# Rests of split weights: an adding transfer issued by GpSimd onto a negative written by ScalarE, in place of subtractions on VectorE and GpSimd

## The chip, the cores and the metric

One core of one Trainium2 chip runs the whole program once per launch. The metric is the device time of that launch in microseconds (us); lower is better.

## The reference

Two blocks on a sequence of 1024 rows of width 1024 (batch 1, depth 1), all in float32. The first normalises x, projects it by one wide matrix, runs two gated linear attentions (chunked) and a cross attention over 256 memory rows, gates the result and projects it back. The second is a convolution block with a gated pointwise product, a depthwise convolution of width 31, a LayerNorm and a second pointwise product, and then a hidden layer. Cut to the products by weights:

```python
proj = rms_norm(x, norm_w) @ w_in                       # 1024 x 6160
mkv = rms_norm(mem, mem_norm_w) @ w_mem_kv              # 1024 x 1024
x = rms_norm(x + (mixed * silu(gate)) @ w_out, final)   # 2048 x 1024
u = hl @ w_pw1 + b_pw1                                  # 1024 x 2048
a, g = split(u); u = dwconv(a * sigmoid(g), w_dw) + b_dw
xl = xl + g1 * (silu(layer_norm(u)) @ w_pw2 + b_pw2)    # 1024 x 1024
xl = xl + g2 * (square(relu(h2 @ w1)) @ w2)             # 1024 x 4096 x 1024
out = rms_norm(xl, final_g)
```

## The kernel before, in words

**Split products.** Each float32 operand of a weight product is split into a high part (the value cast to the type float32r) and a rest (the value less its high part), and the product is three matmuls in float32r: high by high, high by rest, rest by high (`mm3`). Activations are split where they are made. Weights are split after they have been loaded.

**Weight tasks.** All weight products except those of the hidden layer are cut into 92 tasks, `Task`. A task has one weight tile of 128 x 2048 float32 (1 MB; 2176 columns in the two tasks with the low-rank gate). The kinds are `in` (input projection), `out`, `kv` (memory), `pw1` and `pw2`. Each task's generator yields after a quarter of its matmuls (about 24 of 256 columns or 12 of 512), a `kv` task after each of its two halves. The loop at the end of `block_kernel` takes task after task from `W.next()`; after each yield it calls `W.tick` and then `service`.

**Class `Weights`.** Three rings of two buffers each hold the loaded tile (`wst`), its high part (`whi`) and its rest (`wlo`). While a task runs, the tile of the next one is split and the one after it is loaded by SyncE. `plan` writes the split as a list of six entries, `todo`. For each half of the tile (1024 columns), `hi(j)` casts the half to `whi` on ScalarE, and two entries `lo` subtract a quarter each (512 columns) into `wlo`. The helper `rest` picks VectorE or GpSimd for each subtraction by a cost model. The very first tile takes another way (`eager`). `tick(done)` issues entries until their share of the list reaches `done`; `next` flushes what is left. So where an entry stands in the order of its engine is set by the number that the loop hands to `tick`: 1.3 times the share of the task that has been issued (2.0 times in the tasks of `pw2` of the second half).

**Order of the other work.** All other work (scores, recurrences, norms, modulation, the convolution) waits in lanes of steps. `service` issues a step when the model's times for its inputs are due and when the model has VectorE and ScalarE no more than 2.0 and 3.5 us ahead of TensorE (`room`, `LIMITS`). The model (`Model.note`) books each instruction under the name of the issuing engine object; only what SyncE issues is booked as a transfer. Each engine then runs its own list in order.

**Hidden layer.** `hidden_layer` comes last and has its own split (`Operands`). It isn't touched.

Every engine operation passes through one helper, so the profile gives line 217 for all; groups are told apart by tiles. In the profile `ps_d` is the PSUM bank ring of the weight products, `hTh`/`hTl`, `mTh`/`mTl` and `acth`/`actl` are high part and rest of activations, `at` a score tile, `macc` an accumulator of the modulation, `osb` an output of the recurrence, `rs`/`rsb` row statistics, and `orc` a reciprocal.

Of the kernel before, what the change touches and what calls it, by code (L numbers as in the profile page):

```python
# [10 lines left out]
F32 = mybir.dt.float32  # L11
# [4 lines left out]
ALU = mybir.AluOpType  # L16
# [207 lines left out]
class Weights:  # L224
# [26 lines left out]
    def plan(self, fast=False):  # L251
        if not self.staged:
            return
        task, st, n = self.staged.pop(0)
        q = n // 4
        box = {}

        def first():
            box["hi"] = self.pool.tile([P, WB], F32R, tag="whi", name="whi")
            box["lo"] = self.pool.tile([P, WB], F32R, tag="wlo", name="wlo")  # L260
            self.ready.append((task.key, box["hi"], box["lo"]))

        def sc(j):
            v = st[:, j * 1024:(j + 1) * 1024].rearrange("p (k c) -> p k c", c=512)
            self.V.tensor_tensor(v, v, task.scale().unsqueeze(1).to_broadcast([P, 2, 512]), op=ALU.mult)

        if self.eager:
            def eager(j):
                if j == 0:
                    first()  # L270
                c = slice(q * j, q * (j + 1))
                self.V.tensor_copy(box["hi"][:, c], st[:, c])
                e = self.G if j < 2 else self.V
                e.tensor_tensor(box["lo"][:, c], st[:, c], box["hi"][:, c].bitcast(F32), op=ALU.subtract)
            self.todo, self.n_todo, self.eager = [lambda j=j: eager(j) for j in range(4)], 4, False
            return

        def hi(j):
            self.A.copy(box["hi"][:, 2 * q * j:2 * q * (j + 1)], st[:, 2 * q * j:2 * q * (j + 1)])

        def lo(j):
            c = slice(q * j, q * (j + 1))
            self.rest(box["lo"][:, c], st[:, c], box["hi"][:, c].bitcast(F32), fast)

        td = []
        for j in range(2):
            if task.scale is not None:
                td.append(lambda j=j: sc(j))
            td.append(lambda j=j: (first() if j == 0 else None, hi(j)))
            td.append(lambda j=j: lo(2 * j))  # L290
            td.append(lambda j=j: lo(2 * j + 1))
        self.todo, self.n_todo = td, len(td)

    def start(self):
# [65 lines left out]
def block_kernel(ctx, tc, x, mem, w_in, w_up, w_kv, w_out, w_mod, w_pw1, w_pw2, w_dw, w_1, w_2,  # L360
# [837 lines left out]
    def less(out, a, b, eng=None):  # L1198
        n = a.free_size()
        v, g = M.free.get("DVE", 0.0) + n / 800.0, M.free.get("POOL", 0.0) + n / 400.0  # L1200
        (eng or (V if v + GAIN < g else G)).tensor_tensor(out, a, b, op=ALU.subtract)

    class Operands:
# [18 lines left out]
        def lo(self, n, eng=None):  # L1222
            t = self.t[n]
            less(t[:, 1, :], self.val(n), t[:, 0, :].bitcast(F32), eng)
            if self.after:
                self.after(n, t)
# [417 lines left out]
    def hidden_layer():  # L1644
# [26 lines left out]
        for c in range(CHUNKS):  # L1671
            for t in range(NT):
                nxt = (c, t + 1) if t < NT - 1 else (c + 1, 0)
                if nxt[0] < CHUNKS:
                    load_s(*nxt)
                out_group(c, t, B0 + 28 * c + 7 * t)
        assert not plan, sorted(plan)


# [156 lines left out]
    W = Weights((V, A, G, DMA, rest), pw, pick)  # L1836
    done = {}

    def mark(ev, *tiles):
        done[ev] = M.time(*tiles) if tiles else M.last  # L1840
# [48 lines left out]
    def due(n):  # L1889

        if not lanes[n]:
            return None
        st = lanes[n][0]
        if any(r not in done for r in st.req):
            return None
        return max([done[r] for r in st.req] + [M.time(*st.need()) if st.need else 0.0] + banks(st.psum))
# [31 lines left out]
    def service(force=False, kind=None):  # L1928

        any_, more = False, True  # L1930
        while more:
            more = False
            for k, e in enumerate(fifo):
                if later_due(e) <= M.now + SLACK:
                    emit_fifo(k)
                    more = True
                    break
            for n in order():
                d = due(n)
                if d is not None and d <= M.now + SLACK and (force or lanes[n][0].rank in URGENT or room(kind)):  # L1940
                    emit(n)
                    more = True
                    break
            any_ = any_ or more
        if force and not any_:
            c = [(due(n), 1, n) for n in lanes if due(n) is not None] + [(later_due(e), 0, k) for k, e in enumerate(fifo)]
            if not c:
                return False
            _, lane_, n = min(c)
            emit(n) if lane_ else emit_fifo(n)  # L1950
        return True

    while True:
        nxt = W.next()
        if nxt is None:
            break
        task, hi, lo = nxt
        if TRACK:
            TRACK["slots"].append((TRACK["pos"][0], round(M.now, 1), task.key))
        while not all(r in done for r in task.req):  # L1960
            if TRACK:
                print("wait", round(M.now, 1), task.key, [r for r in task.req if r not in done],
                      {n: (len(l), l[0].req, due(n)) for n, l in lanes.items() if l}, len(fifo))
            assert service(True), (task.key, [r for r in task.req if r not in done], [(n, l[0].req) for n, l in lanes.items() if l])
        here = 0.0
        for dt in task.go(hi, lo):
            here += dt
            W.tick(min(1.0, (2.0 if task.key[:2] == ("pw2", 1) else 1.3) * here / task.est))
            service(kind=task.key[0])
        if task.ev is not None:  # L1970
            mark(task.ev)
# [62 lines left out]
def build(nc, arrays, dbg=None):  # L2034
    aps = [nc.dram_tensor(f"in_{n}_dram", arrays[n].shape, mybir.dt.from_np(arrays[n].dtype), kind="ExternalInput").ap()
           for n in _ARGS]
    out = nc.dram_tensor("out_0_dram", (S, D), F32, kind="ExternalOutput").ap()
    with tile.TileContext(nc) as tc:
        block_kernel(tc, *aps, out, dbg=dbg)
# [11 lines left out]
```

## Time and profile before

| | |
|---|---|
| time, median of 2 runs | 2038.71 us (2037.25 to 2040.17) |
| the profiled execution | 2043.66 us, of which the span on the core is 2041.6 us |
| busy share of the span | TensorE 96%, VectorE 74%, ScalarE 45%, GpSimd 40% |
| weight tasks | until about 1395 us; the hidden layer follows |
| transfers issued by GpSimd | none |

The span runs from the first to the last instruction of the core. A share of busy time is a mean over stages with different limits. Matmuls overlap in the profile: the end of one is modelled and lies after the start of the next, so a busy TensorE isn't a TensorE at its peak. Idle time is put down to what ended it.

### The profile page before, as it was taken

The page shows a single profiled execution, that of the slowest core. Times are in us where ns is not written, and L with a number is a line of the kernel's source. Part 1 is how long each engine was busy: PE and PEld are TensorE (multiplying, and loading weights), DVE is VectorE, ACT ScalarE, POOL GpSimd, SP SyncE. Part 2 cuts the span into 40 slices and gives each one's busy share as a digit, 9 for nine tenths or more (in the row PEclk, how much of TensorE's full clock was granted, in tenths as well). Part 3 has the DMA queues.
Part 4 walks back from the last instruction along what each step waited for, and adds up shares of the span by engine and source line. Part 5 has one row for each costly group of instructions (what it writes and reads, how often), then busy time and mean ns, then how long its engine had stood idle before and what let it go on. Part 6 is the DMA issues. An engine that isn't in the chain of part 4 may idle for free.

```text
span 2041.6 us, 29949 instructions
## 1 busy us (share of the span) xinstructions
PE 1952.8 (96%) x10892; PEld 1699.0 (83%) x10892; DVE 1504.7 (74%) x2956; ACT 919.5 (45%) x1793; POOL 811.9 (40%) x743
## 2 busy tenths in 40 slices
PE   8999999999999998999899999999999998899998
PEld 6888898789788887878789999997878886688786
DVE  5799777744667877856757676887888778777876
ACT  6433333444623334334424343335777776433343
POOL 3343334344333443343536343650000003877872
PEclk9999999999999999999999999999999999999999
DMA  5242331333123332322433232331699899776765
GB/s 198 68 159 104 114 114 63 144 124 105 45 101 136 123 109 89 133 83 83 141 133 119 71 119 91 117 132 62 179 300 270 245 263 300 264 285 263 268 250 204
DMA packets 177638, 315.05 MB, mean 154 GB/s; under 512 B 9762, under 2 KB 129442, under 8 KB 163794
## 3 DMA queue, kind: packets, MB, share of 16 engines
q1 hardware_dynamic: 175186, 309.33, 44.8%
q10 hardware_dynamic: 2304, 3.80, 0.5%
q8 instruction: 86, 1.41, 0.3%
q14 instruction: 62, 0.51, 0.1%
HBM read 241.78 MB, written 71.31 MB: 153 GB/s over the span
## 4 chain that ended last, share of the span: by engine, by line
PE 64%; DVE 20%; ACT 5%; DMA 4%; issue 3%; POOL 3%; SPq 0%; DVEq 0%; POOLq 0%; ACTq 0%
PE ps_d L217 38%; PE ps_s L217 20%; PE ps_m L217 7%; DVE macc L217 2%; DVE Q L217 2%; DVE wlo L217 2%; DMA sl<-so 1%; DVE a L217 1%; DVE at L217 1%; DVE tree L217 1%; DMA wlo<-sl 1%; DVE xn L217 1%; POOL wlo L217 1%; DVE zt L217 1%; DVE actl L217 1%
## 5 line engine op out<-in xcount | busy, mean ns | idle before, releaser
L217 POOL TENSOR_TENSOR wlo<-wst,whi 128x512 fp32r<-128x512 f32 (+1 forms) x235 | 335.9, 1444 | 393.0 <-ACT whi L217 387.9
L217 PE MATMUL ps_d<-hTh,whi 128*128 128x512 f32 x576 | 234.7, 407 | 0.0
L217 PE MATMUL ps_d<-hTh,wlo 128*128 128x512 f32 x576 | 227.8, 395 | 0.0
L217 PE MATMUL ps_d<-hTl,whi 128*128 128x512 f32 x576 | 227.5, 395 | 0.0
L217 PE MATMUL ps_d<-whi,acth 128*128 128x256 f32 x768 | 219.4, 286 | 0.5 <-DVE yg L217 0.5
L217 PE MATMUL ps_d<-wlo,acth 128*128 128x256 f32 x768 | 218.3, 284 | 1.2 <-POOL wlo L217 1.2
L217 POOL TENSOR_TENSOR wst<-wst,g 128x512 f32<-128x512 f32 x64 | 93.3, 1476 | 317.0 <-DMA g<-g2d 291.4
L217 PE MATMUL ps_d<-whi,actl 128*128 128x256 f32 x768 | 217.9, 284 | 0.0
L217 ACT CAST whi<-wst 128x1024 fp32r<-128x1024 f32 (+1 forms) x182 | 189.5, 1049 | 48.7 <-PE ps_d L217 42.9
L217 PE MATMUL ps_s<-tm,whi 128*128 128x512 f32 x620 | 191.9, 391 | 5.9 <-ACT ps_s L217 3.2
L217 PE MATMUL ps_s<-hm,tw 128*128 128x512 f32 x768 | 183.1, 393 | 5.5 <-ACT hc L217 3.4
L217 PEld LDWEIGHTS ps_s<-hm,tw 128*128 128x128 f32 x768 | 144.4, 189 | 38.5 <-ACT hc L217 5.3
L217 DVE TENSOR_TENSOR wlo<-wst,whi 128x512 fp32r<-128x512 f32 (+1 forms) x133 | 109.6, 837 | 66.4 <-ACT whi L217 63.3
L217 PEld LDWEIGHTS ps_d<-wlo,acth 128*128 128x128 f32 x768 | 148.0, 193 | 2.0 <-POOL wlo L217 1.7
L217 PEld LDWEIGHTS ps_d<-whi,acth 128*128 128x128 f32 x768 | 148.0, 193 | 1.0 <-issue 1.0
L217 PEld LDWEIGHTS ps_d<-whi,actl 128*128 128x128 f32 x768 | 148.1, 193 | 0.0
L217 PEld LDWEIGHTS ps_s<-tm,whi 128*128 128x128 f32 x620 | 115.6, 188 | 32.7 <-ACT ps_s L217 5.0
L217 DVE COPY_PREDICATED at<-msk,ps_s 128x64 f32<-128x64 uint8 (+1 forms) x704 | 109.2, 245 | 37.1 <-PE ps_s L217 37.0
L217 PEld LDWEIGHTS ps_d<-hTh,whi 128*128 128x128 f32 x576 | 110.3, 191 | 24.3 <-issue 3.3
L217 PEld LDWEIGHTS ps_d<-hTh,wlo 128*128 128x128 f32 x576 | 109.9, 191 | 24.2
L217 PEld LDWEIGHTS ps_d<-hTl,whi 128*128 128x128 f32 x576 | 110.2, 191 | 21.6 <-issue 0.2
L217 PE MATMUL ps_s<-tm,wlo 128*128 128x512 f32 x310 | 121.1, 391 | 4.6 <-DMA wlo<-sl 4.6
(290 smaller groups left out, 4995.3 us busy)
## 6 DMA issues: line engine op xcount, KB each, us to landing
wst<-in_w_in_dram SPq DMA_DIRECT2D x46, 1024.0 KB, 4.8
wst<-in_w_dram SPq DMA_DIRECT2D x32, 1024.0 KB, 6.7
sh<-so SPq DMA_DIRECT2D x112, 256.0 KB, 4.2
sl<-so SPq DMA_DIRECT2D x112, 256.0 KB, 4.0
whi<-sh SPq DMA_DIRECT2D x31, 896.0 KB, 4.8
wlo<-sl SPq DMA_DIRECT2D x31, 896.0 KB, 7.5
wm<-in_w_mod_dram SPq DMA_DIRECT2D x48, 512.0 KB, 6.8
wst<-in_w_pw_dram SPq DMA_DIRECT2D x24, 1024.0 KB, 4.9
```

Source lines behind the costliest of these rows:

```text
L217: r = f(*args, **kw)
```

## The change

The two subtractions of each half are replaced by one multiplication on ScalarE (`less`: the negative of the high part, into `wlo`) and one transfer that GpSimd issues (`lo`: the loaded half is added to what stands in `wlo`). A list still has six entries: cast, negative, transfer, for each half. The factor for `tick` becomes 2.2 in all tasks. The first tile (`eager`) stays as it is.

```diff
+        def less(j):
+            c = slice(2 * q * j, 2 * q * (j + 1))
+            self.A.mul(box["lo"][:, c], box["hi"][:, c].bitcast(F32), -1.0)
+
         def lo(j):
-            c = slice(q * j, q * (j + 1))
-            self.rest(box["lo"][:, c], st[:, c], box["hi"][:, c].bitcast(F32), fast)
+            c = slice(2 * q * j, 2 * q * (j + 1))
+            self.G.dma_start(box["lo"][:, c].bitcast(F32), st[:, c], accum_op=ALU.add)
...
             td.append(lambda j=j: (first() if j == 0 else None, hi(j)))
-            td.append(lambda j=j: lo(2 * j))
-            td.append(lambda j=j: lo(2 * j + 1))
+            td.append(lambda j=j: less(j))
+            td.append(lambda j=j: lo(j))
...
-            W.tick(min(1.0, (2.0 if task.key[:2] == ("pw2", 1) else 1.3) * here / task.est))
+            W.tick(min(1.0, 2.2 * here / task.est))
```

## Rows read from the trace of the kernel before

**Rows 1.** The page, busy time, share of the span and instructions

```profile
PE 1952.8 (96%) x10892; PEld 1699.0 (83%) x10892; DVE 1504.7 (74%) x2956; ACT 919.5 (45%) x1793; POOL 811.9 (40%) x743
```

**Rows 2.** Stretches: start and end, length, busy by engine, clock, DMA share, GB/s

```profile
0.00:20.00 20.00, 11.16 (x69) 10.55 (x70) 11.62 (x33) 12.89 (x36) 7.66 (x20) 1.00 0.76 272
20.00:1395.00 1375.00, 1327.50 (x8154) 1190.20 (x8153) 982.14 (x2182) 547.96 (x1099) 568.70 (x539) 0.98 0.31 110
1395.00:2041.60 646.60, 614.12 (x2675) 498.29 (x2672) 510.92 (x743) 358.61 (x660) 235.49 (x184) 0.99 0.75 244
```

**Rows 3.** Waits of TensorE, 0 to 1395 us: total, times, longest

```profile
PE ps_s L217 <- DVE at L217: 11.3, 4, 4.2
...
PE ps_m L217 <- DVE macc L217: 7.5, 4, 3.4
PE ps_d L217 <- DVE wlo L217: 6.6, 5, 3.4
PE ps_d L217 <- POOL wlo L217: 6.2, 5, 4.5
PE ps_m L217 <- DVE orc L217: 3.0, 1, 3.0
PE ps_m L217 <- DVE osb L217: 2.3, 4, 0.8
```

**Rows 4.** Groups by line: count, busy us, mean ns, idle before

```profile
L217 POOL TENSOR_TENSOR wlo<-wst,whi 128x512 fp32r<-128x512 f32 (+1 forms) x235 | 335.9, 1444 | 393.0 <-ACT whi L217 387.9
L217 ACT CAST whi<-wst 128x1024 fp32r<-128x1024 f32 (+1 forms) x182 | 189.5, 1049 | 48.7 <-PE ps_d L217 42.9
L217 DVE TENSOR_TENSOR wlo<-wst,whi 128x512 fp32r<-128x512 f32 (+1 forms) x133 | 109.6, 837 | 66.4 <-ACT whi L217 63.3
```

**Rows 5.** Tile wlo, VectorE: duration min/median/max, first and last start

```profile
L217 DVE TENSOR_TENSOR wlo<-wst,whi x133: 674/687/1834, 12.7 to 1362.7; 128x512 fp32r<-128x512 f32 x129, 128x544 fp32r<-128x544 f32 x4
```

**Rows 6.** Groups by line and form, GpSimd: busy us, mean ns

```profile
L217 POOL TENSOR_TENSOR rsb<-rs,neghalf 128x1 f32<-128x1 f32 x42 | 26.6, 634 | 3.5
...
L217 POOL TENSOR_TENSOR ors<-rsb,orc 128x4 f32<-128x4 f32 x8 | 1.6, 201 | 0.6
```

**Rows 7.** DMA issues: count, KB each, median us to landing

```profile
wst<-in_w_in_dram SPq DMA_DIRECT2D x46, 1024.0 KB, 4.8
...
wlo<-sl SPq DMA_DIRECT2D x31, 896.0 KB, 7.5
...
wst<-in_w_pw_dram SPq DMA_DIRECT2D x24, 1024.0 KB, 4.9
...
xd<-xn SPq DMA_DIRECT2D x8, 512.0 KB, 2.8
```

**Rows 8.** Timeline, 622 to 631 us, ScalarE and TensorE

```profile
622.00 1.04 ACT L217 CAST whi<-wst 128x1024 fp32r<-128x1024 f32 x1
...
624.32 1.04 ACT L217 CAST whi<-wst 128x1024 fp32r<-128x1024 f32 x1
...
629.06 0.28 PE L217 MATMUL ps_d<-whi,hTh 128*128 128x256 f32 x1
...
630.62 0.28 PE L217 MATMUL ps_d<-wlo,hTh 128*128 128x256 f32 x1
```

**Rows 9.** Timeline, 470 to 474 us, a kv task: ScalarE, GpSimd, TensorE

```profile
470.11 2.00 ACT L217 CAST whi<-wst 128x1024 fp32r<-128x1024 f32 x2
...
471.23 3.05 POOL L217 TENSOR_TENSOR wlo<-wst,whi 128x512 fp32r<-128x512 f32 x2 [9.03 <-ACT whi L217]
...
472.52 0.28 PE L217 MATMUL ps_d<-whi,mTh 128*128 128x256 f32 x1
473.08 0.39 PE L217 MATMUL ps_d<-wlo,mTh 128*128 128x256 f32 x1 [0.28 <-POOL wlo L217]
```

**Rows 10.** Tile whi, ScalarE: duration min/median/max, first and last start

```profile
L217 ACT CAST whi<-wst x182: 1035/1047/1122, 19.5 to 1369.3; 128x1024 fp32r<-128x1024 f32 x180, 128x1088 fp32r<-128x1088 f32 x2
```

## The prediction

> **What bounds the kernel now.** I read the page's busy line first: TensorE is busy for 96% of the span, VectorE for 74%, ScalarE for 45%, GpSimd for 40% [rows 1]. Then the view by stretches, because the change touches only the weight tasks, which end at about 1395 us [rows 2]. Between 20 and 1395 us TensorE is busy for 1327.5 of 1375 us. That leaves 47.5 us of visible idle time as about the most that any relief of other engines can give back; a stall shorter than the matmul still in flight doesn't show, so the true figure is somewhat larger. In that stretch VectorE has 982 us of work, ScalarE 548, GpSimd 569, and the DMA engines are 31% busy. So this is a TensorE-bound stage in which VectorE is the second most loaded engine. Last I read TensorE's waits [rows 3]: rests that come late (`wlo`) cost 6.6 + 6.2 = 12.8 us, and the larger waits for other work of VectorE (`at`, `macc`, `orc`, `osb`) 11.3 + 7.5 + 3.0 + 2.3 = 24.1 us. These 36.9 us are what the change could take away. What it can add is a rest that lands after TensorE wants it.
>
> **What is removed.** 91 lists of four subtractions, 364 of the 235 + 133 = 368 in the trace (the other four are the first tile's) [rows 4]. GpSimd loses 233 x 1.444 = 336 us, VectorE 131 x 0.837 = 110 us. VectorE gains a little more: its shortest subtraction takes 0.674 us, half of them at most 0.687, the longest 1.834 [rows 5], so some are stretched while another engine works. None of this is on TensorE's path except through the waits of [rows 3]. I take half of the 24.1 us as gone (12 us), because VectorE keeps 872 of its 982 us and a score chain stays a chain; the ends are 0 and 24.1.
>
> **What is added on ScalarE.** 182 multiplications of 1024 columns. No row shows this one; the nearest is the cast of the same shape at 1.049 us [rows 4], so 191 us. ScalarE goes from 548 to 739 us of 1375, 54%. I cost the load itself at nothing: it lies beside the matmuls. What waits behind it in ScalarE's order are evacuations of PSUM. After a first quarter the list now puts cast, negative, cast in a row, 3 x 1.05 = 3.1 us; three banks for the weight products give TensorE two more groups of 2.8 us before it would stop. If that cover were gone, each of 91 bursts could cost some tenths of a us, 20 to 30 us in all; this I leave to a rival.
>
> **What is added on GpSimd and the DMA engines.** 182 transfers of 512 KB. In GpSimd's order each waits for its negative, as the subtraction waits for its cast today (387.9 us of idle time [rows 4]); row statistics and key products queue behind it as they do now, but 336 us of subtractions are replaced by 182 short issues. The trace has no transfer issued by GpSimd, and none that adds. Bounds for the step on GpSimd: its smallest operation at 0.20 us and the subtraction at 1.44 us; I take its one-column operation, 0.63 us, because issuing doesn't work through columns [rows 6]. Bounds for issue to landing: a plain 512 KB store at 2.8 us and the slowest common load at 7.5 us; I take the 1 MB loads, 4.8 to 4.9 us, because adding has to read 512 KB twice [rows 7]. So the delay from the end of the negative to the landing, D below, is 0.63 + 4.85 = 5.5 us, between 3.0 and 8.9. On the load of the engines: 31% at 110 GB/s is about 355 GB/s when full, so 1 MB is 2.95 us, and 182 of them are 537 us or 39% of the stretch; 70% in all. That isn't saturated, but a load of weights and an adding transfer will meet often, which the upper bound has to hold.
>
> The Trainium skill, Collectives: The Full Stack, section "The bandwidth ceiling", says that an add in the DMA path isn't slow for its arithmetic but for its two source reads; no run here shows it yet. With DMA: Bandwidth & Descriptors, section "Anatomy of one DMA", whose fit is about 2 us plus the bytes at 436 GB/s, an estimate for 1 MB read is 4.4 us, so D would be 5.0 and the sum below 10 us lower, 2061 us.
>
> **When a rest is due.** Today two entries are issued after the first quarter of a task (1.3 x 0.25 x 6 = 1.95), four after the second and six after the third. Now four are issued after the first quarter (2.2 x 0.25 x 6 = 3.3, rounded up) and all six after the second. So the second negative stands where the second cast stands today, one cast's length at most later; I take 0.4 us after the end of today's second cast (ends 0 and 1.05), since the first three operations mostly fit into idle time of ScalarE. The rest of the second half then lands D later.
>
> An ordinary short task [rows 8]: the second cast ends at 625.36, the negative would end at 625.8, the transfer land at 631.3. TensorE turns to that tile at 629.06 and reads the second half of the rest at 630.62: 0.7 us late.
>
> A memory task (`kv`) has only 48 short matmuls, 5.8 us, and there are four [rows 9]. All six entries come after its first half. The casts start at 470.11; with a negative in between, the first negative ends at 472.2 and its transfer lands at 477.7. TensorE wants it right after 472.52: 5 us late, and the second half another 0.8 us. Today the same place costs 0.28 us. Four of these are 23 us.
>
> I did this for all 91 lists, from the first cast at 19.5 us to the last at 1369.3 [rows 10], against TensorE's first matmul of the next task on each half. The sum of what is late, and the number of late lists: 20 us (10) for D = 3.0, 36 (12) for 4.3, 57 (23) for 5.5, 86 (36) for 6.5, 127 (48) for 7.5, 205 (63) for 8.9. At D = 5.5 the 0.4 us matter by 52 to 70 us. The curve is steep because many tasks run without a break and have 2 to 4 us to spare.
>
> **The sum.** + 57 (late rests) - 12.8 (today's late rests are part of the 57) - 12 (half of VectorE's waits) = + 32 us. The profiled execution took 2043.66 us for a span of 2041.6; it lies 5 us above the median of the runs shown, 2038.71, and the difference is put on the median: 2071 us, 1.6% slower. The hidden layer starts later and runs as before. A measurement of this kernel can tell about 2%, or 41 us, from no change.
>
> **Rivals.**
>
> *The transfers land early.* At D = 3.0 late rests cost 20, and if VectorE's waits go completely the sum is 20 - 12.8 - 24.1 = - 17 us: 2022 us. For it: stores of 512 KB land in 2.8 us [rows 7], and GpSimd is freed. Against it: that store reads its bytes once and isn't issued by GpSimd. To be faster by 41 us, nearly all of the 47.5 us of idle time would have to go.
>
> *The transfers land late.* At D = 7.5, 127 - 12.8 - 12 = + 102 us: 2141 us; at 8.9, 2219 us. For it: two reads and a write of each byte, meetings with the 1 MB loads, and an issue that GpSimd may have to work out for 128 rows. It becomes slower by 2% from the point at which late rests cost 66 us, which is D = 5.9, only 0.4 above what I took.
>
> *The order of the other work suffers.* The model books the transfer under GpSimd and the negatives on ScalarE, and steps wait while ScalarE is 3.5 us ahead. If that holds back score and modulation steps so that the waits of 24.1 us double instead of halving, the sum is 57 - 12.8 + 24.1 = + 68 us: 2107 us. For it: after the first quarter the model sees 2.8 us of new work on ScalarE at once. Against it: VectorE's limit, 2.0 us, is the tighter one today and is relieved.
>
> *The subtraction only changes its name.* If issuing keeps GpSimd as long as two subtractions, 2.9 us, D is 7.7 and the case is that of the late transfers.
>
> **How the numbers follow.** Chances: as forecast (D from 4.3 to 6.5, 2050 to 2100 us) 0.46, early 0.24, late 0.20 (with the changed name), order 0.10. About a third of the forecast's own cases lie beyond D = 5.9, so slower by over 2% has 0.15 + 0.19 + 0.07 = 0.41; faster by over 2% has 0.03, from the early case alone; within 2% the remaining 0.56. The range takes the early end, 2022, and goes up to D = 7.3, at which late rests cost 118 us: 2038.7 + 118 - 25 = 2132, rounded to 2130. Beyond it lie the worst of the late cases.
>
> **What would show it.** TensorE's waits for DMA into `wlo` in the changed kernel should stand near 50 us, with some 5 us at each of the four `kv` tasks; the median from issue to landing of these transfers near 4.9 us; 182 multiplications on ScalarE near 1.05 us; VectorE's waits below 24 us; DMA share near 0.7 in the stretch. I am wrong if the transfers land within 3 us or need over 7, or if TensorE waits for ScalarE's evacuations instead.

## The result and the profile after

The changed kernel takes 2095.04 us (median of 2 runs, 2092.49 and 2097.59) against 2038.71 us: a ratio of 1.0262 with a 95% interval of 1.0231 to 1.0293. It is slower, at the upper end of what was predicted as the likeliest case. The profiled execution took 2092.49 us with a span of 2090.6 us; before it was 2043.66 and 2041.6, so the two traces stand 49 us apart.

The busy line of the page, and the stretch from the end of the first tile to the end of the weight tasks, now at about 1440 us (its columns as in [rows 2]):

```profile
PE 1965.1 (94%) x10892; PEld 1711.1 (82%) x10892; DVE 1325.8 (63%) x2857; ACT 1099.7 (53%) x1975; POOL 596.0 (29%) x660
...
20.00:1440.00 1420.00, 1333.03 (x8127) 1194.84 (x8126) 801.67 (x2080) 727.50 (x1279) 352.78 (x456) 0.97 0.67 174
```

The ends of the stretches, 1395 us in [rows 2] and 1440 here, are round numbers; the last matmul that reads a weight tile's rest starts at 1385.3 us before and at 1434.8 now, so the weight tasks end 49.5 us later and what follows takes as long as it did. Against [rows 1]: VectorE lost 179 us of work, GpSimd 216, ScalarE gained 180; against [rows 2], the DMA share of the stretch went from 0.31 to 0.67. The relief came as intended; yet TensorE, which bounds the stretch, has the same 10,892 matmuls and is busy for 12.3 us longer.

TensorE's waits from 0 to 1440 us, to be held against [rows 3]:

```profile
PE ps_d L217 <- DMA wlo<-wst: 71.8, 27, 11.8
PE ps_m L217 <- DMA wdw<-in_w_dw_dram: 8.2, 1, 8.2
...
PE ps_m L217 <- DVE macc L217: 3.2, 3, 2.4
PE ps_m L217 <- DVE osb L217: 1.0, 3, 0.5
PE ps_s L217 <- DVE at L217: 1.0, 2, 0.5
```

Waits for rests went from 12.8 to 71.8 us. The four waits for VectorE that the prediction counted went from 24.1 to 5.2 us. The load of `wdw` is new in the list: it wasn't waited for before. If all rows of the two views are summed by what was waited for, rests go from 12.8 to 72.1, VectorE's other work from 42.2 to 14.1, other DMA from nothing to 8.2: 55.7 to 95.2 us in all. With TensorE's longer busy time that is 39.5 + 12.3 = 52 us, about the 49 us between the traces.

The new operations, by tile and by DMA issue (count, KB, median us from issue to landing):

```profile
L217 ACT ACTIVATE wlo<-whi x182: 1040/1059/1129, 20.6 to 1418.9; 128x1024 fp32r<-128x1024 f32 x180, 128x1088 fp32r<-128x1088 f32 x2
L217 POOL DMA_DIRECT2D wlo<-wst x182: 850/873/1176, 21.9 to 1420.4; - x182
...
DMA to landing us min/median/max: 4.5/5.1/11.8
```

```profile
wlo<-wst POOLq DMA_DIRECT2D x180, 512.0 KB, 5.1
...
wm<-in_w_mod_dram SPq DMA_DIRECT2D x48, 512.0 KB, 7.7
...
xn<-xd SPq DMA_DIRECT2D x12, 512.0 KB, 9.7
```

The landing is counted from the start of GpSimd's 0.87 us, so that step is inside the 5.1 us. From the end of each negative to its landing I measured, over all 182 pairs in the trace, a median of 5.6 us, a mean of 6.2, a quarter beyond 6.6 and a tenth beyond 9.3. Other loads take longer too: `xn<-xd` needed 6.9 us before, `wm` 6.8.

One memory task, which is the case of [rows 9]. ScalarE, GpSimd, TensorE:

```profile
429.25 1.05 ACT L217 CAST whi<-wst 128x1024 fp32r<-128x1024 f32 x1
430.33 1.06 ACT L217 ACTIVATE wlo<-whi 128x1024 fp32r<-128x1024 f32 x1
...
431.80 0.93 POOL L217 DMA_DIRECT2D wlo<-wst  x1 [2.91 <-ACT wlo L217]
...
431.78 0.28 PE L217 MATMUL ps_d<-mTl,whi 128*128 128x256 f32 x1
436.43 0.58 PE L217 MATMUL ps_d<-mTh,wlo 128*128 128x256 f32 x1 [4.36 <-DMA wlo<-wst]
```

The cast starts at 429.25, the negative ends at 431.39, the transfer is issued at 431.80 and TensorE goes on at 436.43, 5.0 us after the negative. All four memory tasks look like this: 4.36, 4.35, 4.46 and 4.70 us. In the task behind the second there are 4.49 us more, of another kind; they are shown below. The windows of this stretch (column 8 is TensorE's granted clock):

```profile
430.00:480.00 50.00, 36.80 (x177) 31.16 (x176) 13.85 (x21) 25.66 (x35) 10.73 (x16) 0.83 0.74 189
480.00:520.00 40.00, 30.34 (x198) 28.76 (x197) 4.36 (x13) 17.64 (x30) 4.35 (x6) 0.87 0.60 149
```

The granted clock is given as a share of 2.4 GHz and is a mean over the two levels, 2.4 and 1.2 GHz. So where TensorE stood idle, the matmuls behind the wait run slower as well.

The longest wait, 11.79 us, has another history. SyncE, ScalarE, GpSimd and TensorE from 976 to 1002 us:

```profile
976.78 1.99 SPq L217 DMA_DIRECT2D xn<-xd  x4
...
976.14 1.04 ACT L217 CAST whi<-wst 128x1024 fp32r<-128x1024 f32 x1
984.71 1.06 ACT L217 ACTIVATE junk<-xn 128x1024 bf16<-128x1024 f32 x1 [7.53 <-DMA xn<-xd]
...
994.35 1.05 ACT L217 ACTIVATE wlo<-whi 128x1024 fp32r<-128x1024 f32 x1
...
995.80 0.91 POOL L217 DMA_DIRECT2D wlo<-wst  x1 [2.31 <-ACT wlo L217]
...
1000.40 0.80 PE L217 MATMUL ps_d<-wlo,mixh 128*128 128x512 f32 x1 [11.79 <-DMA wlo<-wst]
1001.00 0.63 PE L217 MATMUL ps_d<-whi,mixl 128*128 128x512 f32 x1
1001.43 0.63 PE L217 MATMUL ps_d<-whi,mixh 128*128 128x512 f32 x1
```

The cast of the second half is done at 977.2. Its negative runs only at 994.35, because ScalarE's order has row sums of `xn` between the two, and the first waits 7.53 us for its load; copies of `K` and `gate` follow. Four loads of `xn` were issued from 976.78, and a transfer by GpSimd at the same time; they took 7.9 to 11.2 us to land. Behind the wait matmuls of 512 columns start 0.43 us apart, at a granted clock of 0.50 from 1000 to 1004 us; ordinary ones start 0.23 us apart.

The 4.49 us in the task behind the second memory task have the same history, with a load of `xs` (ScalarE, TensorE):

```profile
447.43 1.03 ACT L217 CAST whi<-wst 128x1024 fp32r<-128x1024 f32 x1
459.19 1.06 ACT L217 ACTIVATE junk<-xs 128x1024 bf16<-128x1024 f32 x1 [10.73 <-DMA xs<-in_x_dram]
...
461.60 1.05 ACT L217 ACTIVATE wlo<-whi 128x1024 fp32r<-128x1024 f32 x1
...
467.66 0.80 PE L217 MATMUL ps_d<-wlo,mixh 128*128 128x512 f32 x1 [4.49 <-DMA wlo<-wst]
```

### The profile page after: what moved, and what is told of

Read it like the earlier page. It is cut to its first block, busy times and chain, and to the rows that moved or that the text cites. A ratio compares the mean times of both kernels' runs of the same rounds, so it can differ in the third digit from the quotient of the medians.

```text
span 2090.6 us, 30079 instructions
## 1 busy us (share of the span) xinstructions
PE 1965.1 (94%) x10892; PEld 1711.1 (82%) x10892; DVE 1325.8 (63%) x2857; ACT 1099.7 (53%) x1975; POOL 596.0 (29%) x660
## 4 chain that ended last, share of the span: by engine, by line
PE 70%; DMA 10%; DVE 8%; ACT 7%; issue 3%; POOL 1%; SPq 0%; ACTq 0%; POOLq 0%; DVEq 0%
PE ps_d L217 41%; PE ps_s L217 23%; PE ps_m L217 7%; DMA wlo<-wst 6%; DMA wlo<-sl 1%; ACT wlo L217 1%; ACT whi L217 1%; DVE zt L217 1%; DVE acc L217 1%; ACT junk L217 1%; DMA wdw<-in_w_dw_dram 1%; DMA xs<-in_x_dram 1%; DVE pg L217 1%; ACT L217 0%; DVE hm L217 0%
## 5 line engine op out<-in xcount | busy, mean ns | idle before, releaser
L217 POOL DMA_DIRECT2D wlo<-wst x182 | 160.2, 882 | 697.8 <-ACT wlo L217 468.9
L217 ACT ACTIVATE wlo<-whi 128x1024 fp32r<-128x1024 f32 (+1 forms) x182 | 192.7, 1059 | 3.3
L217 PE MATMUL ps_d<-wlo,mixh 128*128 128x512 f32 x256 | 103.8, 405 | 25.3 <-DMA wlo<-wst 25.3
```

Of the source, the lines that this page charges most:

```text
L217: r = f(*args, **kw)
```

## The experiments

Theory L: the rests land late, by the time from negative to landing against TensorE's slack, and that is the 56 us. Theory O: the earlier issue and ScalarE's 191 us more upset the order of the other work. Other expectations name their theories themselves. All ratios are to the kernel before, run on the same chip.

| kernel | us | ratio (95%) | waits for rests | VectorE busy | GpSimd busy | TensorE busy |
|---|---|---|---|---|---|---|
| before | 2038.71 | | 12.8 | 1504.7 | 811.9 | 1952.8 |
| changed | 2095.04 | 1.0262 (1.0231 to 1.0293) | 71.8 | 1325.8 | 596.0 | 1965.1 |
| addition on GpSimd | 2108.98 | 1.0334 (1.0314 to 1.0355) | 25.0 | 1511.2 | 892.6 | 1970.3 |
| factor 2.2 alone | 2029.67 | 0.9942 (0.9926 to 0.9958) | 10.1 | 1528.3 | 813.5 | 1942.8 |
| subtractions in memory tasks | 2067.24 | 1.0124 (1.0109 to 1.0140) | 49.1 | 1334.7 | 604.4 | 1957.8 |
| changed, factor 4.4 | 2084.85 | 1.0211 (1.0182 to 1.0241) | 39.8 | 1315.8 | 605.5 | 1969.6 |
| changed, old factors | 2141.67 | one run | 101.8 | 1318.9 | 601.7 | 1976.6 |
| plain copies | 2036.51 | 0.9978 (0.9968 to 0.9989) | 35.9 | 1320.6 | 540.4 | 1950.2 |
| first half only | 2021.51 | 0.9901 (0.9880 to 0.9921) | 17.6 | 1419.4 | 662.1 | 1944.0 |
| transfers cut in two | 2097.94 | 1.0277 (1.0261 to 1.0292) | 71.2 | 1322.3 | 760.1 | 1972.3 |
| first half only, rest on VectorE | 2007.34 | 0.9837 (0.9817 to 0.9856) | 11.3 | 1426.1 | 547.0 | 1937.4 |
| all on VectorE, factor 2.2 | 1994.27 | 0.9777 (0.9761 to 0.9793) | 4.6 | 1520.9 | 496.8 | 1935.9 |
| all on VectorE, old factors | 1996.13 | 0.9785 (0.9768 to 0.9803) | 5.1 | 1526.4 | 503.2 | 1932.0 |

**An addition on GpSimd in place of the transfer.**

```diff
-            self.G.dma_start(box["lo"][:, c].bitcast(F32), st[:, c], accum_op=ALU.add)
+            self.G.tensor_tensor(box["lo"][:, c], st[:, c], box["lo"][:, c].bitcast(F32), op=ALU.add)
```

> The transfer is replaced by one addition of 1024 columns on GpSimd itself; the negatives on ScalarE, the factor 2.2 and the order of the instructions on TensorE, VectorE and ScalarE stay as in the changed kernel. Theory L (the rests land late because the transfer needs about 5.6 us from the end of the negative to its landing): the addition ends about 2.9 us after the negative (two subtractions of 512 columns at 1.44 us), waits for the rest fall from 72 us to about 20 to 25, and the time is about 2035 to 2050 us. Theory O (the order of the other work and the 191 us more on ScalarE cost the time): that is unchanged, so about 2085 to 2095 us.

The waits for rests did what theory L said, 25.0 us, and the time did not: 2109 us. VectorE ran the same 2857 instructions in the same order as in the changed kernel and needed 185 us more for them. Its groups by form in the changed kernel, and then in this one (count, busy us, mean ns):

```profile
L217 DVE TENSOR_TENSOR a<-a 128x256 f32<-128x256 f32 x112 | 57.8, 516 | 1.7
...
L217 DVE TENSOR_TENSOR xl<-ps_d,xl 128x512 f32<-128x512 f32 x64 | 44.1, 688 | 75.4 <-PE ps_d L217 75.1
...
L217 DVE TENSOR_TENSOR pg<-pa,pg 128x256 f32<-128x256 f32 x32 | 15.2, 475 | 32.9 <-ACT pg L217 32.9
```

```profile
L217 DVE TENSOR_TENSOR a<-a 128x256 f32<-128x256 f32 x112 | 83.0, 741 | 1.7
...
L217 DVE TENSOR_TENSOR xl<-ps_d,xl 128x512 f32<-128x512 f32 x64 | 43.7, 686 | 45.0 <-PE ps_d L217 44.9
...
L217 DVE TENSOR_TENSOR pg<-pa,pg 128x256 f32<-128x256 f32 x32 | 37.6, 1176 | 36.2 <-ACT pg L217 36.2
```

Operations with both inputs in SBUF are stretched, the last of these rows from 475 to 1176 ns; one that reads PSUM (`xl<-ps_d`) is not. The Trainium skill, SBUF — State Buffer, section "Who interferes with whom", says that a VectorE instruction with two SBUF inputs contends with a GpSimd instruction that reads SBUF, and that one with at most one doesn't, outside VectorE's two-port modes. The trace agrees, 475 to 1176 ns against 688 to 686. Forms with one SBUF tensor and a scalar for each partition were stretched too (`macc<-wm,scv`, 480 to 839 ns); whether such a mode is the reason isn't shown here. This run was meant to tell the landing from the order of the work; it brought a cost of its own and settles the first half only.

**The factor alone**, in the kernel before:

```diff
-            W.tick(min(1.0, (2.0 if task.key[:2] == ("pw2", 1) else 1.3) * here / task.est))
+            W.tick(min(1.0, 2.2 * here / task.est))
```

> The kernel before with the factor 2.2 alone, subtractions as before. Theory L: the earlier issue alone does no harm; late rests fall from 12.8 us towards 5, so about 2025 to 2040 us. Theory O: issuing casts and rests earlier holds up the other work, and a part of the 56 us shows here, 2055 us or more.

2029.67 us, 12 us faster. The earlier issue does no harm by itself, so the negatives and transfers cost more than the 56 us: about 65 against this kernel.

**Subtractions in the lists issued during memory tasks**, transfers in all others (`quarter` is the old subtraction of 512 columns through `rest`):

```diff
...
+            if short:
+                td.append(lambda j=j: quarter(2 * j))
+                td.append(lambda j=j: quarter(2 * j + 1))
+                continue
...
-            self.plan(task.key[0] in FAST)
+            self.plan(task.key[0] in FAST, task.key[0] == "kv")
```

> The changed kernel, but the lists issued during the four memory tasks use the old quarter subtractions. Theory L: the four waits of 4.4 to 4.7 us there (17.9 us) and about 4.5 us behind them go, and with them the drops of the granted clock to 0.72 to 0.84 in that stretch, so 18 to 30 us less: 2065 to 2077 us. Theory O, or if these waits only hide others: at most 5 us less, 2088 to 2095 us.

2067.24 us: by the ratios 1.38 points, or 28 us, within what theory L gave. The waits for rests fall by 22.7 us. The granted clock of the stretch that showed 0.83 and 0.87 is back at 1.00:

```profile
430.00:480.00 50.00, 49.55 (x323) 44.58 (x321) 24.54 (x32) 27.57 (x40) 22.23 (x21) 1.00 0.66 203
480.00:520.00 40.00, 39.49 (x257) 34.06 (x257) 20.31 (x52) 25.16 (x75) 6.49 (x10) 1.00 0.51 132
```

Half of the loss hung on 4 of 91 lists.

**A factor of 4.4:**

```diff
-            W.tick(min(1.0, 2.2 * here / task.est))
+            W.tick(min(1.0, 4.4 * here / task.est))
```

> The changed kernel with the factor 4.4: all six entries of a list are issued after the first quarter of a task, so the second transfer starts about a quarter of a task (2.7 us) earlier wherever the tile has been loaded by then. Theory L: fewer rests are late, waits for the rest fall from 72 to 30 to 50 us, 2055 to 2075 us. Theory O: three more operations of ScalarE at once (3.1 us) hold up evacuations and scores, so 2095 to 2120 us.

Between the two: 2084.85 us. Its interval and that of the changed kernel overlap, so the times alone don't tell the two kernels apart. Waits for rests fell to 39.8 us, as theory L had it, but new waits came that theory O had named. Its waits of TensorE:

```profile
PE ps_d L217 <- DMA wlo<-wst: 39.8, 22, 8.0
...
PE ps_d L217 <- ACT gate L217: 6.6, 1, 6.6
...
PE ps_m L217 <- ACT prob L217: 2.6, 1, 2.6
PE ps_m L217 <- DVE z L217: 2.6, 1, 2.6
PE ps_d L217 <- DVE yg L217: 2.5, 1, 2.5
```

The largest of these, 6.6 us, isn't the price of a longer burst. It stands where the changed kernel has its 11.79 us, behind the loads of `xn` (ScalarE, TensorE):

```profile
969.37 1.06 ACT L217 ACTIVATE wlo<-whi 128x1024 fp32r<-128x1024 f32 x1
981.55 1.06 ACT L217 ACTIVATE junk<-xn 128x1024 bf16<-128x1024 f32 x1 [11.12 <-DMA xn<-xd]
...
989.59 0.60 ACT L217 ACTIVATE gate<-ps_d 128x512 f32<-128x512 f32 x1
...
990.24 0.79 PE L217 MATMUL ps_d<-whi,mixh 128*128 128x512 f32 x1 [6.63 <-ACT gate L217]
```

The negative now runs ahead of these loads, and the evacuation of `gate` waits behind them. Whether the three waits of 2.5 to 2.6 us come from the bursts was not followed.

**The old factors** in the changed kernel:

```diff
-            W.tick(min(1.0, 2.2 * here / task.est))
+            W.tick(min(1.0, (2.0 if task.key[:2] == ("pw2", 1) else 1.3) * here / task.est))
```

> The changed kernel with the factors of the kernel before (1.3, and 2.0 in the pw2 tasks of the second half): the second negative and its transfer are issued a quarter of a task (about 2.7 us) later. Theory L: that is as if a rest took 8.3 us in place of 5.6; by the sums over the 91 lists the waits for the rest rise from 72 us to about 170 to 190, so 2180 to 2210 us. Theory O (the early issue on ScalarE is what holds up the other work): 2095 us or less.

2141.67 us and 101.8 us of waits in 52 places: the direction of theory L, and its sum much too high, 30 us more in place of about 100 to 118. I had moved every list by the 2.7 us of a short task; why most of that is missing was not followed further.

**Copies in place of additions.** The same transfers in the same order, without the adding:

```diff
-            self.G.dma_start(box["lo"][:, c].bitcast(F32), st[:, c], accum_op=ALU.add)
+            self.G.dma_start(box["lo"][:, c].bitcast(F32), st[:, c])
```

> The changed kernel with transfers that copy and don't add (the rest is then the loaded weight itself: the adding is left out); order and number of transfers are the same. If the second read of an adding transfer sets the landing: the median from issue to landing falls from 5.1 us to 4.0 or less, waits for the rest from 72 to 30 to 40 us, 2045 to 2065 us, and the DMA share falls by a fifth or more. If the issue by GpSimd and a fixed delay set it: the median stays at 4.8 to 5.1 us, waits 60 to 72 us, 2080 to 2095 us.

This run changes nothing but the adding: in its trace TensorE, VectorE, ScalarE and GpSimd run the same instructions in the same order as in the changed kernel. DMA issues and TensorE's waits:

```profile
wlo<-wst POOLq DMA_DIRECT2D x180, 512.0 KB, 2.9
```

```profile
PE ps_d L217 <- DMA wlo<-wst: 35.9, 18, 6.9
```

The landing falls from 5.1 to 2.9 us, GpSimd's step from 0.88 to 0.56 us, the queue's share of the DMA engines from 24.0% to 11.9%, half for the same bytes. The time falls by 58 us to 2036.51, by the ratio 0.2% below the kernel before, though ScalarE still has all 182 negatives and GpSimd all 182 issues. So it is the adding that turns the change into a loss. Between the two traces, 56.8 us apart, the waits for rests fall from 71.8 to 35.9 us, TensorE's busy time falls by 14.9 and the wait for `wdw` by 3.7. This doesn't make the rest of the change free: against the kernel before, the copies have 23 us more of waits for rests, and the relief of VectorE's other waits, 28 us, covers them. The Trainium skill, Collectives: The Full Stack, section "The bandwidth ceiling", puts the price of the add in a ReduceScatter on its two source reads; the doubled share here agrees.

**Transfers for the first half of a tile only**, subtractions for the second half and in memory tasks:

```diff
...
+            if short or j == 1:
+                td.append(lambda j=j: quarter(2 * j))
+                td.append(lambda j=j: quarter(2 * j + 1))
+                continue
             td.append(lambda j=j: less(j))
             td.append(lambda j=j: lo(j))
...
-            self.plan(task.key[0] in FAST)
+            self.plan(task.key[0] in FAST, task.key[0] == "kv")
```

> The first half of each tile by negative and transfer, the second half (and all of the lists issued in memory tasks) by the old quarter subtractions; factor 2.2. Theory L: the first half's rest has half a task more, nearly none is late, and the waits for rests fall below 15 us. Since half of the subtractions are gone, VectorE's waits stay below the 40 us of the kernel with the factor alone: 2015 to 2035 us. Theory O, or if the transfers slow other traffic or the tail: 2050 to 2080 us.

2021.51 us, as theory L had it: where the slack is half a task longer, waits for rests are 14.2 (transfers) + 3.4 (subtractions) us, a little above the 15 expected, and the kernel beats the one before by 1%.

**Each transfer cut in two** of 256 KB:

```diff
-            self.G.dma_start(box["lo"][:, c].bitcast(F32), st[:, c], accum_op=ALU.add)
+            for k in (2 * j, 2 * j + 1):
+                c = slice(q * k, q * (k + 1))
+                self.G.dma_start(box["lo"][:, c].bitcast(F32), st[:, c], accum_op=ALU.add)
```

> The changed kernel with each transfer cut in two of 256 KB, one issued right after the other. If the bytes set the landing: the first of the two lands 3.5 to 4.2 us after its issue, the second at about 5 us, where TensorE wants it a little later; waits for the rest fall from 72 to 40 to 50 us, 2060 to 2075 us. If a fixed delay sets it: the first lands at 4.5 to 5 us and the second 0.9 us after it, waits stay or rise, 2090 to 2110 us.

Bytes do count: the first of two lands 3.9 us after its issue (median over the 182 pairs). But the second lands 5.6 us after that issue, 0.5 us later than the whole transfer did. The wait that was one became two:

```profile
PE ps_d L217 <- DMA wlo<-wst: 71.2, 48, 8.2
```

71.8 us in 27 places became 71.2 in 48, and the time stayed, 2097.94 us.

**First half only, and the remaining subtractions all on VectorE.** This and the next two follow the first experiment's finding.

```diff
-            self.rest(box["lo"][:, c], st[:, c], box["hi"][:, c].bitcast(F32), fast)
+            self.V.tensor_tensor(box["lo"][:, c], st[:, c], box["hi"][:, c].bitcast(F32), op=ALU.subtract)
```

> As the kernel with transfers for the first half only, but its 190 remaining quarter subtractions all on VectorE (84 of them stood on GpSimd). Theory C (VectorE's operations on SBUF stretch while GpSimd subtracts: 449 us of additions on GpSimd went with 185 us more on VectorE for the same instructions, 0.41 us for each): VectorE gains 84 x 0.68 = 57 us of subtractions and is stretched by 125 x 0.41 = 51 us less, about even, and the rests come sooner, since a subtraction takes 0.7 us there and 1.55 us on GpSimd: 2010 to 2022 us. Theory V (VectorE is the second bound, what it is given shows): 2025 to 2040 us.

2007.34 us, below even theory C's range. GpSimd did 84 in the kernel above, two of them the first tile's; VectorE took the other 82 for 7 us more of busy time, 1419.4 to 1426.1.

**All subtractions on VectorE**, no transfers, factor 2.2 (the same edit in the kernel of the factor alone):

> The kernel with the factor 2.2 alone, all subtractions on VectorE, no transfers and no negatives. Theory C: VectorE gains 225 x 0.69 = 155 us of subtractions and is stretched by 340 x 0.41 = 140 us less, so its busy time stays near 1528 us and the time near 2030 us (2020 to 2035); the gain of the kernel with transfers for the first half is then the transfers' own. Theory V: 2040 to 2060 us.

VectorE's busy time is 1520.9 us, below the 1528.3 of the kernel that left 223 of the lists' subtractions to GpSimd (225 with the first tile's two); theory C gave about that number. The time, 1994.27 us, is better than either theory had it, and below that of the kernel with half of the transfers. Busy line and waits:

```profile
PE 1935.9 (97%) x10892; PEld 1691.7 (85%) x10892; DVE 1520.9 (76%) x3182; ACT 918.3 (46%) x1790; POOL 496.8 (25%) x517
```

```profile
PE ps_s L217 <- DVE xs L217: 9.4, 2, 7.6
PE ps_d L217 <- DVE wlo L217: 4.6, 2, 4.2
```

Summed as above, TensorE's waits in the weight tasks fall from 55.7 to 25.9 us and its busy time from 1952.8 to 1935.9: 47 of the 49 us between the spans.

**The same with the old factors**, so that the choice of engine is the only edit of the kernel before:

> The kernel before with all subtractions of the lists on VectorE and nothing else changed (factors 1.3 and 2.0). If the gain of the kernel with all subtractions on VectorE (1994 us) comes from the choice of engine, and the factor gives its 12 us on top as it did alone: 2000 to 2012 us. If the earlier issue is what lets VectorE carry them: 2025 us or more.

1996.13 us. The choice of engine gives all of it, and the factor adds nothing measurable on top; that its 12 us would add was wrong.

## Why the prediction was right in kind and short in size

*The late rests.* The place was right: TensorE waits for `wlo`, in the memory tasks above all, and no operation on ScalarE stands in its place. This was the mis-sized term: 57 us forecast, 71.8 measured. The delay D was not the reason. Its median is 5.6 us against the 5.5 forecast, and 22 of the 27 waits, 60.2 us, hang on transfers that landed 4.8 to 5.9 us after their negative. D has a tail (mean 6.2, longest 12.2 us), but of the 61 transfers that needed more than 6 us from their negative TensorE waited for 5, 11.6 us in all. That the forecast's curve gives about 77 us for a delay of 6.2 is therefore luck. Worked out list by list from the trace, with 5.5 us for every transfer from where its negative really ended, the waits come to 71 us, as measured; with 6.2 us they would be 89.

What failed is the place of the negatives. The prediction put each second one 0.4 us after today's second cast; it asked what waits behind the negatives in ScalarE's order, and not what they wait behind. Three negatives ran 13 to 17 us after the cast of their half: behind the load of `xs`, behind the loads of `xn`, and behind row sums and copies of `prob` with the work on `nz` and `gate`. TensorE waited 4.49, 11.79 and 2.69 us for their transfers, where the prediction's rule, put on the trace of the kernel before, gives 0, 5.1 and 0.4. That is 13.5 of the 15 us that were missing; the other lists come out in sum about as forecast, 52 against 53 us. The plain copies agree: 30.6 of their 35.9 us hang on 13 transfers of at most 3.4 us, an ordinary delay for a copy.

The tail itself goes with transfers that meet others. Of the 182, 72 were issued while a transfer of another queue was under way, and their median from issue to landing is 6.5 us; for the other 110 it is 4.6. Of the 46 that need over 6 us from their issue, 39 are among the 72.

*The parts of D.* I had 0.63 us for GpSimd's step and 4.85 behind it, from the loads of 1 MB. It is about 0.4 us from the negative to the issue and 5.1 us from there, with a step of 0.87 inside. The reason given for the value, two reads of 512 KB, fits the plain copies: 2.9 us in place of 5.1, and half the share of the DMA engines. The bound of 2.8 us was the price of the copy.

*The memory tasks.* 23 us forecast, 17.9 measured at the four and 4.5 in the task behind one. Taking them out gave 28 us, of which waits for rests are 22.7. TensorE's busy time fell by 7.3 us with it, as the granted clock of that stretch came back to 1.00; this the prediction left out.

*The relief of VectorE.* 12 us forecast, 18.9 of the 24.1 measured, and 28 over all of VectorE's waits. I took only the removed subtractions for relief. What remained on VectorE became shorter too: `a<-a` took 620 ns before and 516 after (and 505 with all subtractions on VectorE), and of the 179 us that VectorE lost only 110 were subtractions. So GpSimd's subtractions had been stretching it all along. Its row before:

```profile
L217 DVE TENSOR_TENSOR a<-a 128x256 f32<-128x256 f32 x112 | 69.4, 620 | 1.6
```

*What was not in the sum.* The wait for `wdw`, 8.2 us, and TensorE's 12.3 us of busy time. The latter fits the clock: over the span it fell from 0.987 to 0.975, which in the traces is 55 us at the lower level before and 107 after, with TensorE busy in 45 and 77 of them. With starts 0.43 us apart in place of 0.23, about 15 of these 32 us more would be the clock's (an estimate). Whether the traffic makes the wait for `wdw` stays open: it is 0.6 us with additions on GpSimd and 4.5 with copies, but 5.7 also in the kernel with all subtractions on VectorE and the old factors, which has no such transfers.

*The sum.* Between the profiled executions +49 us stand against +32: rests 15 more, `wdw` 8 and TensorE's busy time 12 more, less 16 for the larger relief over all of VectorE's waits. That makes 51. The medians stand 56 us apart, because the profiled execution lay 5 us above the median before and 2.5 below it after.

*The rivals.* The early landing is out. The deciding point of the late one, 66 us of late rests, was passed by 6 us, and the larger relief (16 us) and the terms that were not in the sum (20 us) about cancel; so the result lies beyond 2%, where within 2% was the likeliest. It was passed through the held negatives and not by a late landing. The change of name is out: GpSimd is held 0.87 us, not 2.9. The order of the other work did not suffer as that rival had it: VectorE's four waits fell to 5.2 us instead of doubling. It was the negatives that suffered from the other work. A kernel with ScalarE's load alone was not run; in the weight tasks of the changed kernel TensorE waits for ScalarE directly for 0.8 us.

## What to carry to other kernels

A step that moves from an engine into an adding transfer is paid in delay, not in busy time: compare the whole chain, from where its first operation will really stand in its engine's order to the landing, against the shortest slack of its consumer, and keep the old form where the slack is short. Ask of each new operation what it waits behind, loads of other work included, and not only what waits behind it. Before work is moved off a loaded VectorE, look at what GpSimd does beside it: here giving VectorE all 364 subtractions in place of 131 made it 22 us busier (1504.7 to 1526.4) and the kernel 2% faster. A factor found for one arrangement is worth trying again in the next: 2.2 gave 12 us in one and nothing in the other.

## What the runs showed of the hardware that was not expected

Additions on GpSimd, 449 us of them, lengthened the same VectorE instructions by 185 us (`pg<-pa,pg` 2.5 times, `tree<-tree` of 128 columns 2.8 times, 293 to 832 ns), and those with an input in PSUM not at all: all of these together took 605 us in the changed kernel and 604 in that run. An adding transfer of 512 KB within SBUF lands after 5.1 us where a copy takes 2.9, occupies GpSimd for 0.88 us where the copy takes 0.56, and takes twice the share of the DMA engines. Issued while a transfer of another queue was under way, the adding one took 6.5 us in place of 4.6 (medians).
